# Weight staging in two buffers of 1152 columns instead of four of 576, in a two-layer hybrid recurrent decoder step

## Chip, cores and metric

The kernel runs on one core of one Trainium2 chip. The metric is the device time of one execution in microseconds (us), lower is better. The engines of the core are named as the profile names them: PE (TensorE: matrix products; PEld is its loading of weights), DVE (VectorE), ACT (ScalarE), POOL (GpSimd) and SP (SyncE, which here issues nearly all transfers). A q behind the name is the engine's queue of issued transfers and waits.

## What is computed

Two decoder layers over 576 tokens (512 of a prompt and 8 times 8 samples), model width 1024. Per layer, cut to what matters here:

```python
h = rmsnorm(x)
P = h @ W_in            # 1024 x 7952: columns of four mixers, then 4 x 1024 gate columns
o_b = mixer_b(P_b)      # four recurrent mixers (HGRN2, GLA, RWKV-7, retention), each 256 wide
x = x + W_out( sum_b sigmoid(G_b) * (o_b @ W_branch[b]) )
x = x + (silu(g) * u) @ W_ffn_out,  where g, u = split(rmsnorm(x) @ W_ffn_in)   # 2 x 2816 wide
```

All weights are float32 in HBM. The products run in float16 with a high and a low part of each operand (three products for one: high by high, high by low, low by high), so every weight tile has to be split on the chip before PE can use it.

## The kernel before

**Staging of a weight.** `wload` brings a block of weight columns (128 columns for all rows of the contraction, 8 groups of 128 rows for a contraction of 1024, 22 for `W_ffn_out`) in steps of four row groups: a tile "raw" of 128 partitions by 512 columns of float32 from the pool `wraw` (four buffers of `GW` = 576 columns), one transfer of 256 KB into it (L220), then ACT writes the high part (L228) and DVE the low part (L229) into a tile `whl` of a ring. The ring "w" has four slots of 2304 bytes a partition, one step each; the rings "rd" and "gd" have slots of 4608 bytes, two steps each. A raw buffer is free again when DVE has read it; a slot of `whl` when the last product that reads it is done.

**Products.** `gemm` (L233) runs three products for each row group; `proj` (L472) does so for the two halves of 288 tokens. A 128-column block of `W_in` is one unit: 48 products in the trace's tile `pb`.

**Order of the mixing stage.** `mix_units` lists the units: those of the mixers first, and between them two groups of eight gate units (g0, g1). `mix` runs them in order; when half 0 of a unit is through, it calls for the next unit's weights, and at each step of a unit it lets the mixers' generators (recurrences, small products) advance a little, so their work lies between the units on all engines. A gate unit m holds its block of `W_in` and, every second time, a block of `W_branch` 256 columns wide for units m and m+1 (L1445: one raw tile and one slot of "w", also used by the next unit). Its 48 `pb` products are followed by 12 products `ub` with the branch weights, and then comes the next unit's block.

**Strassen stages.** The last two gate groups (`last_gates`, eight pairs) and the feed-forward's up projection (`ffn`, blocks 3 to 21) use seven products instead of eight: four sub-blocks a11, a12, a21, a22 of 512 columns are loaded; POOL adds a22 to a21 by a transfer, then `strassen_weights` splits A11, A22, A12 and, after subtractions on POOL, S2 (in a11), S1 (a21), S3 (a22), S4 (a12), one ACT and one DVE instruction each (L1703, L1704). In `last_gates` a11 and a21 lie in raw, a12 and a22 in "w" (four transfers of 256 KB). In `ffn` an odd block lies in the two "rd" slots (two transfers of 512 KB, halves cut from them); an even block in three raw buffers and one "w" slot.

**Output projection and down projection.** `out_proj` runs blocks 0 to 3 with weights in "w", loads blocks 4 to 7 into "gd" and the feed-forward's first three block pairs (`ffn_weights`, into "w", "gs" and "r2"), while the blocks' results pass through `add_x` on DVE and ACT; `norm_half` then waits for all of them (L442). The down projection (`xb` products, 22 row groups a block) loads each block with rings ("w", "w", "w", "w", "rd").

**Who sets the order.** Each engine works its list in order. The lists are made when the kernel is built, by a scheduler that starts instructions in program order of priority as their inputs and buffers come free in its own model of the time; on the chip an instruction that waits blocks all that stand behind it on its engine.

Of the kernel before, what the change touches and what calls it, by code (L numbers as in the profile page):

```python
# [10 lines left out]
F32 = mybir.dt.float32  # L11
F16 = mybir.dt.float16
I32 = mybir.dt.int32
AF = mybir.ActivationFunctionType
# [20 lines left out]
C_RW = 64  # L35
C_GL = 128
GLA_TAU = 16.0
GW = 576
RINGS = {"u": 23, "e": 6, "gs": 6, "gt": 8, "gq": 5, "gd": 4, "rd": 2, "rs": 6, "r2": 4, "r1": 3, "rk": 2, "rq": 6, "w": 4}
SIZE = {"u": 2304, "e": 1152, "gs": 2304, "gt": 1152, "gq": 512, "gd": 4608, "rd": 4608, "rs": 2304, "r2": 2304, "w": 2304,  # L40
        "r1": 1024, "rk": 1536, "rq": 512}
PS = {"b": 4, "g": 2, "r": 2}
PACE = {"rw": ("rw", "g3", "g3", 140), "hg": ("hg", "g0", "g0", 64), "gl": ("gl", "rt", "g1", 64),
# [131 lines left out]
class Net:  # L175
    def __init__(self, ctx, tc, t):
        self.tc, self.nc, self.io = tc, tc.nc, t
        nc = self.nc

        def pool(name, bufs, **k):  # L180
            return ctx.enter_context(tc.tile_pool(name=name, bufs=bufs, **k))

        self.cp = pool("const", 1)
        self.wp = pool("wraw", 4)
        self.gp = pool("misc", 1)
        self.dr = pool("dram", 2, space=bass.MemoryType.DRAM)
        self.rings = {n: pool("ring_" + n, b) for n, b in RINGS.items()}
        self.pss = {n: pool("ps_" + n, b, space=PSUM) for n, b in PS.items()}
# [19 lines left out]
    def wload(self, pieces, nk, ncols, rings=("w",)):  # L208


        nc = self.nc
        step = GW // ncols
        tiles, parts = [], []
        for g, k0 in enumerate(range(0, nk, step)):
            kn = min(step, nk - k0)
            n = kn * ncols
            raw = self.wp.tile([128, GW], F32, tag="raw", name="raw")
            rv = raw[:, :n].rearrange("p (k c) -> p k c", k=kn)
            for ap, off, w in pieces:
                nc.sync.dma_start(out=rv[:, :, off:off + w],  # L220
                                  in_=ap[128 * k0:128 * (k0 + kn)].rearrange("(k p) c -> p k c", p=128))
            if not parts:
                ring, rings = rings[0], rings[1:] or rings
                c = SIZE[ring] // (4 * GW)
                hl = self.t(ring, [128, c, 2, GW], "whl", F16)
                parts = [hl[:, i] for i in range(c)]
            hl = parts.pop(0)
            nc.scalar.activation(hl[:, 0, :n], raw[:, :n], AF.Copy, scale=WS)  # L228
            nc.vector.scalar_tensor_tensor(hl[:, 1, :n], raw[:, :n], WS, hl[:, 0, :n], op0=MUL, op1=SUB)  # L229
            tiles.append(hl[:, :, :n].rearrange("p a (k c) -> p a k c", k=kn))  # L230
        return lambda k: (tiles[k // step][:, 0, k % step], tiles[k // step][:, 1, k % step])

    def gemm(self, ps, w, ks, c0, m, rhs, step=4):  # L233

# [1258 lines left out]
    def last_gates(self, l):  # L1493
# [3 lines left out]

        def load(bi, m):
            c = COL_GATE + 1024 * bi + 128 * m
            a = []  # L1500
            for i in range(4):
                r = [128, 4, 128]
                a.append(self.t("w", r, "sraw") if i % 2 else self.wp.tile([128, GW], F32, tag="raw", name="raw")[
                    :, :512].rearrange("p (k c) -> p k c", k=4))
                nc.sync.dma_start(out=a[i], in_=t["w_in"][l][512 * (i % 2):512 * (i % 2) + 512, c + 128 * (i // 2):c + 128 * (
                    i // 2) + 128].rearrange("(k p) c -> p k c", p=128))
            return a

        def branch(bi, m):

# [251 lines left out]
    def ffn(self, l):  # L1762
# [21 lines left out]
        def load(m):  # L1784
            q = []
            for o in (0, DFF):
                src = t["w_ffn_in"][l][:, o + 128 * m:o + 128 * m + 128]
                if m % 2:
                    a = self.t("rd", [128, KT, 128], "sraw")
                    nc.sync.dma_start(out=a, in_=src.rearrange("(k p) c -> p k c", p=128))  # L1790
                    q += [a[:, :4], a[:, 4:]]
                    continue
                for i in range(2):
                    if o and i:
                        a = self.t("w", [128, 4, 128], "sraw")
                    else:
                        a = self.wp.tile([128, GW], F32, tag="raw", name="raw")[:, :512].rearrange("p (k c) -> p k c", k=4)
                    nc.sync.dma_start(out=a, in_=src[512 * i:512 * i + 512].rearrange("(k p) c -> p k c", p=128))
                    q.append(a)
            return q  # L1800

        self.sw = {}
# [34 lines left out]
        def weights(m, rings=("w",)):  # L1837
            return self.wload([(t["w_ffn_out"][l][:, 128 * m:128 * m + 128], 0, 128)], nm, 128, rings)
# [6 lines left out]
            self.add_x(m, half, ps, l + 1 < DEPTH, l + 1 == DEPTH and m == KT - 1)  # L1845
        for m in range(6):
            self.load_x(m)
            w = weights(m, ("w", "w", "w", "w", "rd"))
            for half in range(2):
                down(m, w, half)  # L1850
        for m in (6, 7):
            self.load_x(m)
        ws = [weights(6, ("gd",)), weights(7, ("w", "w", "w", "w", "gd"))]
        if l + 1 < DEPTH:
            down(6, ws[0], 0)
            down(7, ws[1], 0)
# [97 lines left out]
```

## Time and profile before

| | us |
|---|---|
| median of three runs | 2204.15 (2200.36 to 2207.76) |
| the profiled execution | 2207.72 |
| its span, first to last instruction | 2205.9 |
| PE busy | 2039.1 |
| DVE busy | 1636.6 |
| ACT busy | 1081.3 |
| POOL busy | 682.3 |

The profile is of one execution. About 2 us of its time lie outside the span. The layers are alike in the trace: layer 0 lasts until about 1103 us and layer 1 from there on. In layer 0, mixing with its first two gate groups ends near 517 us, the last gates near 661, the output projection near 720, the up projection near 973.

### The profile page before, as it was taken

Reading aid. Unit: us, or ns where it says so; the run is one execution under the profiler, and the core shown is the slowest. Engines: PE = TensorE matmul, PEld = TensorE weight load, DVE = VectorE, ACT = ScalarE, POOL = GpSimd, SP = SyncE. Lnnn points to the kernel's source line nnn. Section 1 sums busy time; section 2 is a strip of 40 time slices with the busy share of each in tenths; the row PEclk is TensorE's granted clock in tenths of the full one; section 3 lists DMA queues with packets and bytes.
Section 4 is the critical chain, followed back from the end, with each engine's and each line's share of the span. In section 5 each row is a group of like instructions: output and inputs, shape, how many; then the busy total and the mean of one; then the engine's idle time right before and its main releaser. Section 6 shows DMA issues by size and latency. Waiting matters only on the chain.

```text
span 2205.9 us, 42236 instructions
## 1 busy us (share of the span) xinstructions
PE 2039.1 (92%) x15754; PEld 1612.3 (73%) x15754; DVE 1636.6 (74%) x3409; ACT 1081.3 (49%) x2524; POOL 682.3 (31%) x889
## 2 busy tenths in 40 slices
PE   7989999998888899999999889989998988999998
PEld 5767787786676677777777778768776766777776
DVE  7889667768785899863488986586788779998441
ACT  6554546345444555442466355453645465554332
POOL 2223222146550544320012142213465316443000
PEclk9999999999999999999999999999999999999999
DMA  6312224333435344343421222242343443443331
GB/s 181 84 41 62 58 58 110 77 83 92 116 98 177 80 116 120 87 135 103 122 68 46 58 62 60 73 111 62 87 120 88 131 141 97 111 116 87 121 106 51
DMA packets 373498, 209.59 MB, mean 95 GB/s; under 512 B 59810, under 2 KB 360410, under 8 KB 373292
## 3 DMA queue, kind: packets, MB, share of 16 engines
q1 hardware_dynamic: 365516, 192.73, 31.6%
q0 software_dynamic: 7776, 14.16, 3.6%
q8 instruction: 124, 2.03, 0.4%
q14 instruction: 82, 0.67, 0.1%
HBM read 173.72 MB, written 16.59 MB: 86 GB/s over the span
## 4 chain that ended last, share of the span: by engine, by line
PE 47%; DVE 28%; ACT 8%; issue 7%; DMA 5%; POOL 3%; SPq 1%; DVEq 0%; ACTq 0%; POOLq 0%
PE pb L243 5%; PE pb L242 5%; PE pb L241 5%; PE xb L243 4%; PE xb L242 4%; PE xb L241 4%; DVE hA L1704 4%; DVE hS L1704 3%; DVE sc L1745 2%; DVE fy L1776 2%; DVE whl L229 2%; DVE su L1745 2%; PE fsS L1731 2%; PE fsS L1729 2%; PE fsS L1730 2%
## 5 line engine op out<-in xcount | busy, mean ns | idle before, releaser
L241 PE MATMUL pb<-h,whl 128*128 128x288 f16 (+1 forms) x1504 | 435.8, 290 | 4.4 <-ACT h L464 2.2
L243 PE MATMUL pb<-h,whl 128*128 128x288 f16 (+1 forms) x1504 | 435.5, 290 | 3.2 <-DVE whl L229 3.1
L242 PE MATMUL pb<-h,whl 128*128 128x288 f16 (+1 forms) x1504 | 436.0, 290 | 0.6 <-DVE h L465 0.4
L229 DVE SCALAR_TENSOR_TENSOR whl<-raw,whl 128x512 f16<-128x512 f32 (+1 forms) x352 | 253.8, 730 | 134.3 <-ACT whl L228 132.2
L242 PEld LDWEIGHTS <-whl 128*128 128x128 f16 (+1 forms) x2784 | 275.4, 99 | 88.0 <-issue 13.5
L243 PEld LDWEIGHTS <-whl 128*128 128x128 f16 (+1 forms) x2784 | 275.1, 99 | 88.0 <-issue 12.7
L241 PEld LDWEIGHTS <-whl 128*128 128x128 f16 (+1 forms) x2784 | 277.2, 100 | 76.6 <-issue 3.6
L228 ACT ACTIVATE whl<-raw 128x512 f16<-128x512 f32 (+1 forms) x352 | 213.3, 618 | 168.2 <-PE pb L243 51.9
L243 PE MATMUL xb<-fa,whl 128*128 128x288 f16 x704 | 201.3, 286 | 0.0
L242 PE MATMUL xb<-fa,whl 128*128 128x288 f16 x704 | 201.3, 286 | 0.0
L241 PE MATMUL xb<-fa,whl 128*128 128x288 f16 x704 | 201.3, 286 | 0.0
L1729 PE MATMUL fsA<-h,hA 128*128 128x288 f16 x432 | 124.3, 288 | 14.9 <-DVE gu L1550 10.8
L1729 PE MATMUL fsS<-st,hS 128*128 128x288 f16 x456 | 132.6, 291 | 5.9 <-ACT hS L1703 5.9
L1731 PE MATMUL fsS<-st,hS 128*128 128x288 f16 x456 | 132.4, 290 | 0.4 <-DVE hS L1704 0.3
L1730 PE MATMUL fsS<-st,hS 128*128 128x288 f16 x456 | 132.5, 291 | 0.0
L1731 PE MATMUL fsA<-h,hA 128*128 128x288 f16 x432 | 124.2, 288 | 1.7 <-DVE hA L1704 1.6
L1730 PE MATMUL fsA<-h,hA 128*128 128x288 f16 x432 | 124.3, 288 | 0.0
L1707 POOL TENSOR_TENSOR raw<-raw 128x512 f32<-128x512 f32 x52 | 79.0, 1520 | 134.2 <-DVE hA L1704 129.7
L1729 PEld LDWEIGHTS <-hS 128*128 128x128 f16 x864 | 85.7, 99 | 35.9 <-ACT hS L1703 13.7
L1704 DVE SCALAR_TENSOR_TENSOR hA<-sraw,hA 128x512 f16<-128x512 f32 x110 | 103.1, 945 | 10.6 <-ACT hA L1703 10.6
L1707 POOL TENSOR_TENSOR sraw<-sraw 128x512 f32<-128x512 f32 x60 | 89.7, 1499 | 51.4 <-DVE hA L1704 45.7
L1731 PEld LDWEIGHTS <-hS 128*128 128x128 f16 x864 | 85.7, 99 | 24.8 <-DVE hS L1704 2.6
(486 smaller groups left out, 5257.8 us busy)
## 6 DMA issues: line engine op xcount, KB each, us to landing
raw<-in_w_in SPq DMA_DIRECT2D x208, 256.0 KB
sraw<-in_w_ffn_in SPq DMA_DIRECT2D x40, 512.0 KB
raw<-in_w_ffn_out SPq DMA_DIRECT2D x80, 256.0 KB
raw<-in_w_ffn_in SPq DMA_DIRECT2D x78, 256.0 KB
x<-xd SPq DMA_DIRECT2D x32, 288.0 KB
raw<-sraw POOLq DMA_DIRECT2D x34, 256.0 KB, 3.3
sraw<-in_w_in SPq DMA_DIRECT2D x32, 256.0 KB
raw<-in_w_out SPq DMA_DIRECT2D x32, 256.0 KB
```

What stands on the lines that cost most here:

```text
L228: nc.scalar.activation(hl[:, 0, :n], raw[:, :n], AF.Copy, scale=WS)
L229: nc.vector.scalar_tensor_tensor(hl[:, 1, :n], raw[:, :n], WS, hl[:, 0, :n], op0=MUL, op1=SUB)
L241: nc.tensor.matmul(ps, wh, hi, start=i == 0, stop=False)
L242: nc.tensor.matmul(ps, wh, lo, start=False, stop=False)
L243: nc.tensor.matmul(ps, wl, hi, start=False, stop=i == len(ks) - 1)
L1704: nc.vector.scalar_tensor_tensor(hl[:, 1], a, WS, hl[:, 0], op0=MUL, op1=SUB)
L1707: nc.gpsimd.tensor_tensor(dst, a, b, op=op)
L1729: nc.tensor.matmul(ps, w[a][:, 0, k], hi, start=k == 0, stop=False)
L1730: nc.tensor.matmul(ps, w[a][:, 0, k], lo, start=False, stop=False)
L1731: nc.tensor.matmul(ps, w[a][:, 1, k], hi, start=False, stop=k == 3)
L1745: nc.vector.tensor_tensor(o, a, p, op=ADD)
L1776: nc.vector.scalar_tensor_tensor(y, u, PH * AS, sg, op0=MUL, op1=MUL)
```

## The change

The staging pool has two buffers of 1152 columns instead of four of 576, and the ring "w" two slots of 4608 bytes instead of four of 2304; both take the same memory as before. `wload` takes up to 1152 columns in a step: eight row groups of 128 columns (all of a 1024-row block) in one transfer of 512 KB, and nine, nine and four row groups of `W_ffn_out` instead of five steps of four and one of two. The split is one ACT and one DVE instruction for a whole step where the ring's slot holds it ("w", "rd", "gd"), and several of 512 columns where it doesn't ("gs", "r2"). A block of `W_branch` (512 columns) stays one step, and takes a whole raw buffer and a whole slot of "w". In the Strassen stages a11 and a12 share one buffer, a21 and a22 another, each with one transfer of 512 KB: in `last_gates` one raw and one "w", in `ffn` both "rd" slots for odd blocks as before and both raw buffers for even ones. The products and the Strassen splits are the same.

```diff
-GW = 576
-RINGS = {... "w": 4}
-SIZE = {... "w": 2304,
+GW = 1152
+RINGS = {... "w": 2}
+SIZE = {... "w": 4608,
...
-        self.wp = pool("wraw", 4)
+        self.wp = pool("wraw", 2)
...
-        step = GW // ncols
-        tiles, parts = [], []
-        for g, k0 in enumerate(range(0, nk, step)):
-            kn = min(step, nk - k0)
-            n = kn * ncols
+        tiles = []
+        for k0 in range(0, nk, GW // ncols):
+            k1 = min(k0 + GW // ncols, nk)
             raw = self.wp.tile([128, GW], F32, tag="raw", name="raw")
...
-            if not parts:
-                ring, rings = rings[0], rings[1:] or rings
-                c = SIZE[ring] // (4 * GW)
-                hl = self.t(ring, [128, c, 2, GW], "whl", F16)
-                parts = [hl[:, i] for i in range(c)]
-            hl = parts.pop(0)
-            nc.scalar.activation(hl[:, 0, :n], raw[:, :n], AF.Copy, scale=WS)
-            nc.vector.scalar_tensor_tensor(hl[:, 1, :n], raw[:, :n], WS, hl[:, 0, :n], op0=MUL, op1=SUB)
+            ring, rings = rings[0], rings[1:] or rings
+            size = SIZE[ring] // 4
+            for o in range(0, k1 - k0, size // ncols):
+                kn = min(size // ncols, k1 - k0 - o)
+                hl = self.t(ring, [128, 2, size], "whl", F16)[:, :, :kn * ncols].rearrange(...)
+                src = rv[:, o:o + kn]
+                nc.scalar.activation(hl[:, 0], src, AF.Copy, scale=WS)
+                nc.vector.scalar_tensor_tensor(hl[:, 1], src, WS, hl[:, 0], op0=MUL, op1=SUB)
+                tiles += [(hl[:, 0, k], hl[:, 1, k]) for k in range(kn)]
...
 # last_gates.load
+            for i in range(2):
+                a = self.t("w", [128, KT, 128], "sraw") if i else self.wp.tile(...)[:, :1024]...
+                nc.sync.dma_start(out=a, in_=t["w_in"][l][:, c + 128 * i:c + 128 * i + 128]...)
+                q += [a[:, :4], a[:, 4:]]
...
 # ffn.load
+                a = self.t("rd", [128, KT, 128], "sraw") if m % 2 else self.wp.tile(...)[:, :1024]...
+                nc.sync.dma_start(out=a, in_=src.rearrange("(k p) c -> p k c", p=128))
+                q += [a[:, :4], a[:, 4:]]
...
-            w = weights(m, ("w", "w", "w", "w", "rd"))
+            w = weights(m, ("w", "w", "rd"))
...
-        ws = [weights(6, ("gd",)), weights(7, ("w", "w", "w", "w", "gd"))]
+        ws = [weights(6, ("gd",)), weights(7, ("w", "w", "gd"))]
```

## Rows read from the trace of the kernel before

**Rows 1.** The page: span, and busy time of each engine.

```profile
span 2205.9 us, 42236 instructions
PE 2039.1 (92%) x15754; PEld 1612.3 (73%) x15754; DVE 1636.6 (74%) x3409; ACT 1081.3 (49%) x2524; POOL 682.3 (31%) x889
```

**Rows 2.** Stretches: us, busy us (instructions) of each engine, clock, DMA share, GB/s.

```profile
250.00:350.00 100.00, 98.91 (x778) 81.28 (x776) 61.93 (x173) 45.11 (x156) 27.76 (x59) 1.00 0.24 62
660.00:720.00 60.00, 53.35 (x411) 41.10 (x409) 35.95 (x69) 29.36 (x56) 6.75 (x8) 0.94 0.56 171
760.00:850.00 90.00, 87.08 (x708) 69.01 (x706) 87.49 (x141) 47.95 (x100) 43.23 (x34) 1.00 0.44 115
972.00:1106.00 134.00, 133.84 (x1091) 106.58 (x1089) 53.79 (x102) 43.76 (x82) 1.80 (x2) 1.00 0.42 126
```

**Rows 3.** Splits by form: busy us, mean ns | idle before; the third from 250 to 300 us.

```profile
L228 ACT ACTIVATE whl<-raw 128x512 f16<-128x512 f32 x332 | 205.2, 627 | 162.4 <-PE pb L243 49.5 <-DMA raw<-in_w_ffn_out 32.6 <-PE xb L243 23.6
L228 ACT ACTIVATE whl<-raw 128x256 f16<-128x256 f32 x16 | 6.5, 406 | 3.4 <-DMA raw<-in_w_ffn_out 3.4
L229 DVE SCALAR_TENSOR_TENSOR whl<-raw,whl 128x512 f16<-128x512 f32 x11 | 7.6, 688 | 2.2 <-ACT whl L228 2.0
L229 DVE SCALAR_TENSOR_TENSOR whl<-raw,whl 128x256 f16<-128x256 f32 x16 | 6.7, 421 | 2.1 <-ACT whl L228 2.0
```

**Rows 4.** Timeline of the shortest passage from one gate unit to the next.

```profile
288.41 0.29 PE L243 MATMUL pb<-h,whl 128*128 128x288 f16 x1
...
288.79 0.63 ACT L228 ACTIVATE whl<-raw 128x512 f16<-128x512 f32 x1 [0.46 <-ACT le L1110]
...
289.45 0.69 DVE L229 SCALAR_TENSOR_TENSOR whl<-raw,whl 128x512 f16<-128x512 f32 x1 [0.20 <-ACT whl L228]
...
290.45 0.29 PE L241 MATMUL pb<-h,whl 128*128 128x288 f16 x1
```

**Rows 5.** Timeline of PE, the longest such passage: its first and last product.

```profile
320.76 0.29 PE L243 MATMUL pb<-h,whl 128*128 128x288 f16 x1
...
325.12 0.29 PE L241 MATMUL pb<-h,whl 128*128 128x288 f16 x1
```

**Rows 6.** Waits of PE, whole trace: us in total, times, longest us.

```profile
PE rps L442 <- DVE sq L436: 12.7, 3, 6.8
PE fsS L1729 <- ACT hS L1703: 12.5, 4, 3.3
PE pb L243 <- DVE whl L229: 3.1, 3, 1.3
PE pb L241 <- ACT whl L228: 2.1, 2, 1.4
```

**Rows 7.** Chain of waits, 655 to 725 us: start us, us, what.

```profile
676.64 3.60 DMA raw<-in_w_out
...
688.10 5.59 DMA raw<-in_w_ffn_in
...
695.70 3.23 DMA raw<-in_w_ffn_in
...
700.53 3.80 DMA raw<-in_w_ffn_in
...
708.55 1.34 PE rps L442 x2
```

**Rows 8.** Issues of L220 from 676.6 to 700.5 us.

```profile
L220 SPq DMA_DIRECT2D raw<-in_w_ffn_in x11: 367/367/384, 682.7 to 699.5; - x11
L220 SPq DMA_DIRECT2D raw<-in_w_out x5: 367/368/384, 676.6 to 681.7; - x5
```

**Rows 9.** Chain of waits, 925 to 960 us, and 2025 to 2042 us.

```profile
948.49 2.91 DMA raw<-in_w_ffn_out
...
951.42 0.64 ACT whl L228
...
2032.46 2.79 DMA raw<-in_w_ffn_out
```

**Rows 10.** Timeline of SP's queue, 0 to 35 us: issues.

```profile
18.42 0.33 SPq L345 DMA_DIRECT2D prow<-in_attn_norm_w  x1
...
30.70 2.78 SPq L220 DMA_DIRECT2D raw<-in_w_in  x4
```

**Rows 11.** Waits of ACT, 560 to 660 us.

```profile
ACT hA L1703 <- DMA sraw<-in_w_in: 1.4, 2, 1.0
```

More of the change, by code (lines that the diff above doesn't have):

```diff
@@ L37 @@
 GLA_TAU = 16.0
-GW = 576
-RINGS = {"u": 23, "e": 6, "gs": 6, "gt": 8, "gq": 5, "gd": 4, "rd": 2, "rs": 6, "r2": 4, "r1": 3, "rk": 2, "rq": 6, "w": 4}
-SIZE = {"u": 2304, "e": 1152, "gs": 2304, "gt": 1152, "gq": 512, "gd": 4608, "rd": 4608, "rs": 2304, "r2": 2304, "w": 2304,
+GW = 1152
+RINGS = {"u": 23, "e": 6, "gs": 6, "gt": 8, "gq": 5, "gd": 4, "rd": 2, "rs": 6, "r2": 4, "r1": 3, "rk": 2, "rq": 6, "w": 2}
+SIZE = {"u": 2304, "e": 1152, "gs": 2304, "gt": 1152, "gq": 512, "gd": 4608, "rd": 4608, "rs": 2304, "r2": 2304, "w": 4608,
         "r1": 1024, "rk": 1536, "rq": 512}
@@ L211, in wload @@
         nc = self.nc
-        step = GW // ncols
-        tiles, parts = [], []
-        for g, k0 in enumerate(range(0, nk, step)):
-            kn = min(step, nk - k0)
-            n = kn * ncols
+        tiles = []
+        for k0 in range(0, nk, GW // ncols):
+            k1 = min(k0 + GW // ncols, nk)
             raw = self.wp.tile([128, GW], F32, tag="raw", name="raw")
-            rv = raw[:, :n].rearrange("p (k c) -> p k c", k=kn)
+            rv = raw[:, :(k1 - k0) * ncols].rearrange("p (k c) -> p k c", c=ncols)
             for ap, off, w in pieces:
-                nc.sync.dma_start(out=rv[:, :, off:off + w],
-                                  in_=ap[128 * k0:128 * (k0 + kn)].rearrange("(k p) c -> p k c", p=128))
-            if not parts:
-                ring, rings = rings[0], rings[1:] or rings
-                c = SIZE[ring] // (4 * GW)
-                hl = self.t(ring, [128, c, 2, GW], "whl", F16)
-                parts = [hl[:, i] for i in range(c)]
-            hl = parts.pop(0)
-            nc.scalar.activation(hl[:, 0, :n], raw[:, :n], AF.Copy, scale=WS)
-            nc.vector.scalar_tensor_tensor(hl[:, 1, :n], raw[:, :n], WS, hl[:, 0, :n], op0=MUL, op1=SUB)
-            tiles.append(hl[:, :, :n].rearrange("p a (k c) -> p a k c", k=kn))
-        return lambda k: (tiles[k // step][:, 0, k % step], tiles[k // step][:, 1, k % step])
+                nc.sync.dma_start(out=rv[:, :, off:off + w], in_=ap[128 * k0:128 * k1].rearrange("(k p) c -> p k c", p=128))
+            ring, rings = rings[0], rings[1:] or rings
+            size = SIZE[ring] // 4
+            for o in range(0, k1 - k0, size // ncols):
+                kn = min(size // ncols, k1 - k0 - o)
+                hl = self.t(ring, [128, 2, size], "whl", F16)[:, :, :kn * ncols].rearrange("p a (k c) -> p a k c", c=ncols)
+                src = rv[:, o:o + kn]
+                nc.scalar.activation(hl[:, 0], src, AF.Copy, scale=WS)
+                nc.vector.scalar_tensor_tensor(hl[:, 1], src, WS, hl[:, 0], op0=MUL, op1=SUB)
+                tiles += [(hl[:, 0, k], hl[:, 1, k]) for k in range(kn)]
+        return lambda k: tiles[k]
     def gemm(self, ps, w, ks, c0, m, rhs, step=4):
@@ L1499, in load @@
             c = COL_GATE + 1024 * bi + 128 * m
[L1500 to L1507, printed above, removed]
+            q = []
+            for i in range(2):
+                a = self.t("w", [128, KT, 128], "sraw") if i else self.wp.tile([128, GW], F32, tag="raw", name="raw")[
+                    :, :1024].rearrange("p (k c) -> p k c", k=KT)
+                nc.sync.dma_start(out=a, in_=t["w_in"][l][:, c + 128 * i:c + 128 * i + 128].rearrange("(k p) c -> p k c", p=128))
+                q += [a[:, :4], a[:, 4:]]
+            return q
         def branch(bi, m):
@@ L1787, in load @@
                 src = t["w_ffn_in"][l][:, o + 128 * m:o + 128 * m + 128]
[L1788 to L1799, printed above, removed]
+                a = self.t("rd", [128, KT, 128], "sraw") if m % 2 else self.wp.tile([128, GW], F32, tag="raw", name="raw")[
+                    :, :1024].rearrange("p (k c) -> p k c", k=KT)
+                nc.sync.dma_start(out=a, in_=src.rearrange("(k p) c -> p k c", p=128))
+                q += [a[:, :4], a[:, 4:]]
             return q
```

## Prediction

> **What bounds the kernel.** Read the page's busy times first: PE is busy for 2039.1 of 2205.9 us, 92%, DVE for 74%, ACT for half [rows 1]. So at most 167 us are PE's idle time, and a change pays by closing gaps in PE or costs by opening them. Next, the table by stretch shows that stages differ [rows 2]: in the gate units (250 to 350 us) PE idles for 1.1 us of 100 while DVE has 38 us to spare; in the down projection (972 to 1106) it idles for 0.2 of 134; in the Strassen stage of `ffn` (760 to 850) DVE is as full as PE, 97%; around the output projection (660 to 720) PE idles for 6.7 of 60 and the transfers move most, 171 GB/s. Then the waits of PE: those for a staged weight (pb on whl) sum to 5.2 us in the whole trace, less than the 12.7 us of three waits for the sums of squares and the 12.5 us of four waits for a high part hS [rows 6]. The chains of waits show what stands behind these two: transfers into raw [rows 7, 9]. So the weights are hidden nearly everywhere now. The change keeps bytes, products and Strassen splits; it changes how late a split can begin and how long it lasts.
>
> **Durations after.** From 256 to 512 columns the ACT split grows from 406 to 627 ns, the DVE split from 421 to 688 (the row of the gate units, where POOL disturbs little) [rows 3]. The lines through these points give 1.07 us and 1.22 us for 1024 columns; a fixed part of 0.185 and 0.154 us is saved by each merged pair. The splits fall from 352 to 192 an engine (a layer has 46 blocks of `W_in`, two steps each before and one after, 8 of `W_branch` unchanged, 16 to 8 in `out_proj`, 12 to 10 in `ffn_weights`, 48 to 24 in the down projection): 160 x 0.154 = 25 us of DVE and 160 x 0.185 = 30 us of ACT.
>
> **1. Fewer instructions.** 48 of the 160 lie in the down projection, where PE has no gap to give back [rows 2]. The other 112 save 17 us of DVE in stages in which PE idles for about a tenth at most, so about a tenth of it comes through: take -2 us; bounds -17 (all of it on the path) and 0. The Trainium skill, in "VectorE: DVE Perf Modes", section on the TRN2 errata, says that operations on SBUF pay a fixed latency for each instruction and that larger tiles amortize it. The rows agree that there is a fixed part; by that rule alone the kernel would gain up to the 17 us.
>
> **2. Gate units: the cover of the split shrinks.** Before, "w" has four slots: a block takes two, the branch weights one, so one is always free for half of the next block. After, block and branch fill both slots. The next block's split can't begin until the last of the 48 products pb is done, and it needs ACT and then DVE for the whole 1024 columns before the third product can start. That is 0.04 (the wait) + 1.07 + 0.03 + 1.22 + 0.1 to PE, and between ACT's end and DVE's start some 0.3 us pass while DVE finishes another instruction (0.03 us at best, 289.42 to 289.45 [rows 4]); less the two products that need the high part alone, 0.25: about 2.5 us. The cover is what PE does from the last pb product to the next unit's first: 12 ub products and what the mixers have ready. The shortest such passage lasts 1.75 us (288.70 to 290.45) [rows 4], the longest 4.07 (321.05 to 325.12) [rows 5]. I read all 15 of layer 0: five lie under 2.5 us, at 1.75, 1.9, 2.0, 2.4 and 2.45, short by 2.0 us together; layer 1 repeats them. Scatter of half a us in ACT's and DVE's response adds about one more a layer: take +6 us for both layers. Bounds: 0, if the scheduler finds other products to put there; and 32 passages x (2.5 - 12 x 0.123, the branch products alone at the pitch of the down projection, 134 us over 1091 products [rows 2]) = +33 us. What queues behind the waiting split on ACT is the mixers' next work and the evacuation of half 1, which DVE's gate product needs. On the side of this term the Trainium skill, "Perfetto Trace Analysis", section "Optimizing Scalar/DVE Operations", says that where ScalarE and VectorE aren't saturated but cause bubbles on other engines, breaking instructions up may let work finish sooner; this is the opposite edit, in a stage where they aren't saturated [rows 2].
>
> **3. Output projection: two buffers of 512 KB in flight instead of four of 256 KB.** From 676.64 to 700.53 us, 16 transfers of 256 KB start [rows 7, 8]: 1 MB in 5.97 us. A buffer's round is landing, ACT, DVE, issue. After, landing of 512 KB isn't shown; it lies between the 3.23 us of a lone 256 KB and the 5.59 us of the slowest in a full queue [rows 7]; I take 4.4, nearer to the middle. With 1.07 + 1.22 + 0.5 of waits the round is 7.2 us for two buffers, 1 MB. The stretch has 10 blocks, 5 MB, so it can end 6 us later a layer. The late end shows today: the norm's sum starts at 708.55 [rows 7] after 12.7 us of PE waits in three places [rows 6], because `add_x` on DVE and ACT stands behind splits that wait for transfers. But the lists are made anew with the new durations, and the feed-forward weights aren't needed before 720: take +2 us a layer, +4; bounds -4 (the order puts `add_x` first) and +12.
>
> **4. First down blocks amid the Strassen products.** At 948.49 and 2032.46 us a transfer into a just freed raw buffer is waited for by ACT, behind it the next hS [rows 9]: two of the four waits in [rows 6], near 3 us each. After, block 20 holds both raw buffers until its S4 split, so down weights are staged later, past this place, and the first is needed only at 973. Take -3 (one of the two goes, or both by half); bounds -6 and, if 4.4 us of landing are waited for in place of 2.9, +3.
>
> **5. Last gates and even blocks of `ffn`.** A buffer pair is free after S4 instead of S2, one or two splits later, and lands as 512 KB. The odd blocks of `ffn` work like this already, in the stretch that is 97% busy. In the last gates only 1.4 us of ACT's waits are for these transfers [rows 11]: take +1; bounds 0 and +8 (a us for each of eight pairs).
>
> **6. Start.** The parameter rows sit in a raw buffer from 18.42 us on, and the loads of the fourth unit stand behind them on SP at 30.70 [rows 10]. With two buffers they wait for the whole second block's split instead of half of it. With that and the 5.2 us of pb waits [rows 6], which longer splits stretch: +1.5; bounds 0 and +5.
>
> The down projection costs nothing: a block's first slot is free 13 row groups, 39 x 0.123 = 4.8 us, before the next block, and nine groups are split in 1.2 + 1.4 us; DVE and ACT are busy for 40% and 33% there [rows 2]. If that cover went, 16 passages would pay 1 to 2 us each.
>
> **Sum.** -2 + 6 + 4 - 3 + 1 + 1.5 = +7.5 us against the profiled execution's 2207.72 us (span 2205.9 and 2 us around it). That execution stands 3.6 us above the median of the runs, so for a median I put 2204.2 + 7.5 = 2212.
>
> **Rivals.**
> (a) *The cover holds.* PE fills the passages with mixers' products, and the re-made lists absorb term 3. For it: ten of 15 passages are longer than 2.5 us; against it: PE's gaps there are already so small that little is ready to be moved. Terms 2 and 3 fall to 0: -2 - 3 + 2.5, about 2202.
> (b) *Faster: the fixed cost pays.* In the mixers' stretch DVE and ACT are what PE's small products wait for, and there each merged pair shortens the queue; with all of term 1 (-17), term 4 at its -6, terms 2 and 3 at half (+5) and +2.5 of the rest, -15.5: 2189; with 10 of the 17, 2196. It decides if more than half of DVE's saving comes through to PE. Against it: the saving is 1.5% of DVE's time, spread thin.
> (c) *Two buffers serialize.* A transfer can't start while both are being split, and SP, which waits in order, holds back states and stores too. Terms 2 and 3 go to their ends, +33 and +12, or to two thirds of them, with -2, -3 and +2.5 of the rest: 2231 to 2247. For it: around the output projection the transfers already move 171 GB/s and set the pace; against it: elsewhere they move 62 to 126 GB/s [rows 2].
> That the larger transfers move no faster by themselves is inside the forecast: each row of 128 columns remains a run of 512 bytes.
>
> **Chances.** What a measurement can tell from no change is about 0.3%, 6.6 us. Forecast 0.45, own range 2204 to 2222, of which 0.30 lies above 2210.8 and 0.15 within; (a) 0.20, 0.14 within and 0.06 faster; (b) 0.17, faster; (c) 0.18, slower. Faster 0.23, same 0.29, slower 0.48. The range 2192 to 2236 takes in the forecast and (a), the nearer half of (b) and a third of (c).
>
> **What would show it.** Term 2: new PE waits pb on whl (DVE, ACT) of 0.3 to 1 us between 256 and 338 and between 430 and 500 us. Term 3: the sum's wait at L442 longer than 6.8 us at the longest. Term 4: no wait for hS near 952 and 2035. Term 1: 192 splits on either engine, near 1.07 and 1.22 us. The prediction is wrong if PE's waits for whl stay near 5 us (then the cover held), if the wait at L442 shrinks, or if the down projection's stretch opens gaps.

## The result

| | before | after |
|---|---|---|
| median of four runs each, us | 2204.97 | 2232.09 (2229.36 to 2232.8) |
| ratio | | 1.0123 (95% interval 1.0103 to 1.0143) |
| the profiled execution, us | 2207.72 | 2232.7 |

The changed kernel is slower by 1.2%, 27 us. The forecast was 2212 in a range of 2192 to 2236: the direction is right, the time lies inside the range, but the sum of the terms was +7.5 us and the true one is more than three times that. It lies above the forecast's own range (2204 to 2222), at the lower end of rival (c).

The page of the profile after, busy times and the two groups of splits:

```profile
span 2230.9 us, 41166 instructions
PE 2041.7 (92%) x15754; PEld 1610.3 (72%) x15754; DVE 1622.5 (73%) x3249; ACT 1058.7 (47%) x2364; POOL 680.9 (31%) x889
...
L226 DVE SCALAR_TENSOR_TENSOR whl<-raw,whl 128x1024 f16<-128x1024 f32 (+2 forms) x192 | 225.7, 1180 | 139.1 <-ACT whl L225 139.1
L225 ACT ACTIVATE whl<-raw 128x1024 f16<-128x1024 f32 (+2 forms) x192 | 184.4, 966 | 203.5 <-PE xb L240 45.0
```

Against [rows 1], PE is busy for 2.6 us more, and its idle time grew from 166.8 to 189.2 us: the loss is idle time of PE. DVE (-14 us) and ACT (-23 us) work less, as was meant, and the kernel is slower all the same.

PE's waits after, the largest groups and those of the prediction (engine, line <- what came last: us in total, times, longest; a line number after is 3 or 4 below that of before):

```profile
PE rps L439 <- DVE sq L433: 16.7, 4, 8.3
PE gps L730 <- DVE rw_ab L720: 10.5, 2, 6.1
PE fb L238 <- DVE fy L1772: 9.4, 4, 3.6
PE fsA L1725 <- ACT bhl L1512: 9.1, 4, 2.8
PE pb L240 <- DVE whl L226: 8.8, 8, 1.8
...
PE fsS L1725 <- ACT hS L1699: 8.6, 5, 3.3
```

Against [rows 6]: PE waits 4.0 us longer for the sums of squares and 3.9 us less for hS; for staged weights (with the 3.0 us of L238 on ACT) it waits 11.8 in place of 5.2 us. The group of bhl, the split of branch weights in the last gates, is new.

**Where the 25 us went.** The nine stages are cut at products that every version has: the first pb (end of the start), the first ub (g0 begins), the 96th, 97th and 192nd ub (g0 ends, g1 begins and ends), the first ob, fb and xb, the last xb. "Last gates" holds the mixers' tail too. For each kernel profiled here, the difference from the profile before, in us, both layers added:

| kernel | start | mixers 1 | g0 | mixers 2 | g1 | last gates | output proj. | up proj. | down proj. | sum |
|---|---|---|---|---|---|---|---|---|---|---|
| before (length) | 14.1 | 469.0 | 170.6 | 182.2 | 176.5 | 293.2 | 114.4 | 507.6 | 267.2 | 2194.8 |
| after | +2.9 | +4.4 | +2.7 | +4.2 | +0.7 | +11.3 | +1.5 | -2.6 | 0 | +25.1 |
| control of before | +0.4 | -0.2 | 0 | +0.7 | -0.7 | +0.1 | -0.6 | -3.5 | 0 | -3.9 |
| control of after | +1.8 | +5.1 | +2.4 | +4.0 | +0.6 | +10.0 | +2.1 | -3.4 | 0 | +22.5 |
| "w" alone | +0.3 | +2.9 | +3.5 | -0.8 | +0.7 | +8.4 | -1.5 | -6.0 | 0 | +7.4 |
| raw alone | +2.1 | +9.1 | 0 | -1.6 | +0.8 | +8.6 | +4.1 | -6.4 | 0 | +16.7 |
| raw alone, in halves | +0.8 | +6.5 | 0 | -0.2 | -0.3 | +12.7 | +2.7 | -4.2 | 0 | +17.9 |
| after, in halves | +0.4 | +3.9 | +3.8 | +1.0 | +1.1 | +11.7 | -0.2 | -2.3 | 0 | +19.3 |
| after, splits in halves | +1.5 | +6.1 | +3.5 | -0.6 | +1.5 | +11.3 | -1.1 | +0.1 | 0 | +22.2 |
| after, transfers in halves | +2.2 | +4.0 | +2.4 | +5.1 | +0.3 | +5.0 | +2.6 | -3.5 | 0 | +18.0 |
| after, own quarters | +2.0 | +4.4 | +2.7 | +4.8 | 0 | +8.5 | +1.4 | -4.0 | 0 | +19.8 |
| before, transfers of 128 KB | -0.2 | +2.8 | 0 | -0.1 | -0.3 | -2.5 | -9.3 | -3.1 | 0 | -12.7 |
| before, five of "w" | +1.1 | +0.9 | +1.6 | +3.9 | +3.8 | +11.9 | -7.6 | +7.6 | 0 | +23.2 |
| before, five of raw | +1.2 | +4.5 | 0 | 0 | -1.8 | +7.5 | -9.9 | -7.2 | 0 | -5.6 |

These are single executions, and some stand off the medians of their kernels: that of before by 3 to 6 us, mostly in the up projection, as its control shows, and that of the changed kernel in halves by 6 us. So a column is read against the control's row, and the sum of a row can miss by this much what the medians in the next section give.

Three readings of the trace after. The start, its chain of waits (start us, us, what):

```profile
4.47 7.50 DMA raw<-in_w_in
...
11.99 1.07 ACT whl L225
...
13.08 1.23 DVE whl L226
14.31 0.38 DVE xdg L319
...
14.73 1.34 PE rps L328 x2
```

The first norm's instruction xdg stands behind the first block's split on DVE, and that waits for 512 KB beside the input's transfers. Before, the chain was 5.14, 0.64 and 0.69 us for 256 KB, and this sum started at 11.87.

The last gates of layer 0: the whole stage and two parts of it, first before, then after (us, busy us of PE, PEld, DVE, ACT, POOL, granted clock, DMA share, GB/s):

```profile
517.20:663.00 145.80, 128.75 (x993) 100.38 (x992) 116.48 (x224) 72.92 (x170) 80.69 (x81) 0.98 0.43 110
560.00:588.00 28.00, 26.42 (x190) 19.48 (x188) 20.19 (x39) 14.69 (x30) 14.48 (x16) 1.00 0.50 126
632.20:647.40 15.20, 13.42 (x109) 10.56 (x108) 13.57 (x25) 8.70 (x19) 8.74 (x7) 1.00 0.28 82
```

```profile
526.50:679.20 152.70, 132.80 (x994) 101.69 (x993) 124.44 (x221) 73.03 (x165) 80.50 (x81) 0.96 0.40 106
570.00:601.40 31.40, 28.03 (x190) 20.10 (x187) 20.19 (x39) 13.67 (x28) 15.38 (x17) 0.95 0.54 136
645.90:663.50 17.60, 14.95 (x109) 11.21 (x108) 16.49 (x27) 8.51 (x18) 8.43 (x7) 0.90 0.26 76
```

Of the 6.9 us, 2.9 are idle time of PE and 4.0 are slower products: as many of them, at a granted clock of 0.96 in place of 0.98. DVE is busy for 8 us more with three instructions fewer. The two parts hold most of the loss: 3.4 us at the end of the mixers' tail, where DVE's busy time is the same, and 2.4 us in a passage from one pair to the next. This passage, on PE's timeline after (start us, us, instruction, in brackets the idle time before it):

```profile
648.57 0.40 PE L1725 MATMUL fsA<-h,hA 128*128 128x288 f16 x1 [2.65 <-ACT bhl L1512]
...
651.40 0.44 PE L1725 MATMUL fsA<-h,hA 128*128 128x288 f16 x1
651.64 0.34 PE L1726 MATMUL fsA<-h,hA 128*128 128x288 f16 x1
651.82 0.29 PE L1727 MATMUL fsA<-h,hA 128*128 128x288 f16 x1
```

PE stood still for 2.65 us; the products behind it start 0.24 us apart instead of 0.12, the clock granted being the lower level, 1.2 GHz, until about 651.6. That adds some 1.5 us to the gap. What stands ahead on DVE at that place, and POOL's instructions beside it (timelines: start us, us, instruction):

```profile
639.80 1.62 DVE L1700 SCALAR_TENSOR_TENSOR hA<-raw,hA 128x512 f16<-128x512 f32 x1
641.35 1.76 DVE L1700 SCALAR_TENSOR_TENSOR hA<-sraw,hA 128x512 f16<-128x512 f32 x1
643.03 0.44 DVE L1741 TENSOR_TENSOR su<-sp,fsS 128x288 f32<-128x288 f32 x1
643.39 1.61 DVE L1700 SCALAR_TENSOR_TENSOR hS<-raw,hS 128x512 f16<-128x512 f32 x1
...
645.28 0.68 DVE L1700 SCALAR_TENSOR_TENSOR hS<-sraw,hS 128x512 f16<-128x512 f32 x1
```

```profile
639.60 1.27 POOL L1703 TENSOR_TENSOR raw<-sraw,raw 128x512 f32<-128x512 f32 x1 [2.10 <-DVE hA L1700]
640.95 1.60 POOL L1703 TENSOR_TENSOR raw<-raw 128x512 f32<-128x512 f32 x1
643.18 1.27 POOL L1703 TENSOR_TENSOR sraw<-sraw,raw 128x512 f32<-128x512 f32 x1 [0.62 <-DVE hA L1700]
```

The next pair's splits stand between DVE's evacuations su; those with one of POOL's subtractions beside them take 1.6 to 1.8 us, the one without 0.68.

### The profile page after: what moved, and what is told of

Read it like the earlier page. It is cut to its first block, busy times and chain, and to the rows that moved or that the text cites. A ratio compares the mean times of both kernels' runs of the same rounds, so it can differ in the third digit from the quotient of the medians.

```text
span 2230.9 us, 41166 instructions
## 1 busy us (share of the span) xinstructions
PE 2041.7 (92%) x15754; PEld 1610.3 (72%) x15754; DVE 1622.5 (73%) x3249; ACT 1058.7 (47%) x2364; POOL 680.9 (31%) x889
## 4 chain that ended last, share of the span: by engine, by line
PE 43%; DVE 31%; ACT 9%; issue 8%; POOL 5%; DMA 4%; SPq 1%; DVEq 0%; POOLq 0%; ACTq 0%
DVE hA L1700 4%; PE xb L240 4%; PE xb L239 4%; PE xb L238 4%; PE pb L239 4%; PE pb L240 4%; PE pb L238 4%; DVE hS L1700 3%; DVE whl L226 3%; DVE sc L1741 2%; DVE fy L1772 2%; DVE su L1741 2%; PE fsS L1727 2%; PE fsS L1725 1%; PE fsS L1726 1%
## 5 line engine op out<-in xcount | busy, mean ns | idle before, releaser
L238 PE MATMUL pb<-h,whl 128*128 128x288 f16 (+1 forms) x1504 | 434.4, 289 | 5.3 <-ACT whl L225 3.0
L239 PEld LDWEIGHTS <-whl 128*128 128x128 f16 (+1 forms) x2784 | 275.5, 99 | 93.1 <-issue 17.9
L238 PEld LDWEIGHTS <-whl 128*128 128x128 f16 (+1 forms) x2784 | 277.2, 100 | 77.0 <-issue 4.4
L226 DVE SCALAR_TENSOR_TENSOR whl<-raw,whl 128x1024 f16<-128x1024 f32 (+2 forms) x192 | 225.7, 1180 | 139.1 <-ACT whl L225 139.1
L225 ACT ACTIVATE whl<-raw 128x1024 f16<-128x1024 f32 (+2 forms) x192 | 184.4, 966 | 203.5 <-PE xb L240 45.0
L238 PE MATMUL xb<-fa,whl 128*128 128x288 f16 x704 | 201.3, 286 | 0.0
L1703 POOL TENSOR_TENSOR raw<-raw 128x512 f32<-128x512 f32 x70 | 105.4, 1508 | 126.1 <-DVE hA L1700 124.7
L1725 PE MATMUL fsS<-st,hS 128*128 128x288 f16 x456 | 130.4, 286 | 0.9 <-ACT hS L1699 0.9
L1727 PE MATMUL fsS<-st,hS 128*128 128x288 f16 x456 | 130.4, 286 | 0.6 <-DVE hS L1700 0.6
L1726 PE MATMUL fsS<-st,hS 128*128 128x288 f16 x456 | 130.4, 286 | 0.0
L1725 PEld LDWEIGHTS <-hS 128*128 128x128 f16 x864 | 85.7, 99 | 31.7 <-ACT hS L1699 10.0
L1700 DVE SCALAR_TENSOR_TENSOR hS<-raw,hS 128x512 f16<-128x512 f32 x104 | 96.5, 931 | 15.1 <-ACT hS L1699 14.6
L1107 ACT ACTIVATE le<-le 128x64 f32<-128x64 f32 (+2 forms) x248 | 56.6, 274 | 104.1 <-DVE le L1104 102.6
```

The costliest lines, as they stand in the source:

```text
L225: nc.scalar.activation(hl[:, 0], src, AF.Copy, scale=WS)
L226: nc.vector.scalar_tensor_tensor(hl[:, 1], src, WS, hl[:, 0], op0=MUL, op1=SUB)
L238: nc.tensor.matmul(ps, wh, hi, start=i == 0, stop=False)
L239: nc.tensor.matmul(ps, wh, lo, start=False, stop=False)
L1107: nc.scalar.activation(e, e, AF.Exp, scale=sign)
L1700: nc.vector.scalar_tensor_tensor(hl[:, 1], a, WS, hl[:, 0], op0=MUL, op1=SUB)
```

## The experiments

Theory A: the 27 us come from the buffers, namely from steps of double length (landing, splits) or from fewer, shared buffers that go free late. Rival B: from the lists, which are made anew with each edit and can fall well or badly. Medians beside their kernel before, run with them on one chip (2202.42 for the first four, then 2201.3, then 2202.04).

### "w" alone

```diff
-RINGS = {... "w": 4}   SIZE = {... "w": 2304,
+RINGS = {... "w": 2}   SIZE = {... "w": 4608,
# raw stays 4 x 576; down projection: rings "w", "w", "rd"
# last_gates: a12 and a22 as halves of one slot of "w", four transfers
+            lo = self.t("w", [128, 2, 4, 128], "sraw")
```

> Only the ring "w" is changed (two slots of 4608 bytes); raw stays four buffers of 576 columns, each with its own transfer of 256 KB and its own split into half of a slot. If the two slots of "w" are the cost, most of the 27 us is here: 2222 to 2232. If the raw buffers are (their number, and the transfers and splits of double length that they bring), this kernel stands near the one before: 2204 to 2211, with the gate units between 253 and 338 us as long as before (85.0 us, against 86.2 in the changed kernel), since the first half's split needs only 0.63 + 0.69 us after the last pb product. If the re-made lists alone decide, the time can be anything from 2190 to 2230, and the stages that lose are not the ones that lost before (mixers and last gates).

Measured: 2216.61, ratio 1.0065 (1.0050 to 1.0080), half of the loss. The gate units are longer, g0 by 3.5 us, which I had not expected here: with halves the split should have fitted under the cover. The last gates lose 8.4, the start nothing.

### Raw alone

```diff
-        self.wp = pool("wraw", 4)      # of 576
+        self.wp = pool("wraw", 2)      # of 1152, "w" stays 4 x 2304
# a step is 8 row groups: one transfer, two splits into two slots of "w"
# last_gates: a11 and a12 share a raw buffer, a21 and a22 have a slot of "w" each
```

> Only the raw pool is changed (two buffers of 1152 columns, transfers of 512 KB); "w" stays four slots of 2304 bytes, so a block's split is two ACT and two DVE instructions into two slots. If the raw buffers are the cost: 2220 to 2232, with the start still late (the first norm's sum at 13.5 us or later, against 11.87 before and 14.73 in the changed kernel; the 512 KB land at 12 us, and the first product needs only one half's split) and the last gates 4 us or more longer a layer than 149.4 us. If "w" is the cost: 2205 to 2212. If the lists alone decide: anything from 2190 to 2230.

Measured: 2224.55, ratio 1.0102 (1.0085 to 1.0118). Start late as expected (the first sum at 14.00), g0 at 0. The two parts alone cost 14 and 22 us, both together 27: they overlap.

### The changed kernel in halves

```diff
-                nc.sync.dma_start(out=rv[:, :, ...], in_=ap[128 * k0:128 * k1]...)
+                for ka in range(k0, k1, 512 // ncols): nc.sync.dma_start(...)   # 256 KB each
...
-                nc.scalar.activation(hl[:, 0], src, ...); nc.vector.scalar_tensor_tensor(hl[:, 1], src, ...)
+                for p in halves: the same two on hl[:, :, p], src[:, p]        # 512 columns each
# last_gates and even blocks of ffn: two transfers for each buffer
```

> The changed kernel's buffers (two raw of 1152 columns, two slots of 4608 bytes), but each buffer is filled by transfers of 256 KB and split by instructions of 512 columns. If the length of a transfer and of a split is the cost, this gives most back: 2206 to 2214, the start within 0.5 us of before (first norm's sum at about 12 us). If the number of buffers and the late release of a whole one is the cost, it stays at 2224 to 2236: the fixed part of 160 more splits an engine comes back, and a buffer still goes free only after both halves. If the lists alone decide: anything from 2190 to 2236.

Measured: 2220.89, ratio 1.0089 (1.0073 to 1.0105), between the two expectations. It is 18.5 us above its kernel before, so of the 27 us length costs about a third: nearly all of the start (first sum at 12.23) and most of the second mixers' stretch. Two thirds stay, with steps of the old size in shared buffers.

### A control of before

```diff
         nc.vector.memset(self.eps[:, 1:2], LN_EPS)
+        nc.vector.memset(self.eps[:, 1:2], LN_EPS)
```

> A control: the kernel before with one memset of 128 x 1 elements on VectorE, issued twice instead of once at the very start. By itself it costs under 0.1 us, but the lists of all engines are made anew from it. If the order in the lists is robust, 2202 to 2208 (no change). If re-made lists move the time by themselves, it differs from 2205 by 5 to 15 us in either direction, and a part of the 27 us of this size can't be put down to buffers.

Measured: 2202.09, ratio 0.9996 (0.9987 to 1.0005). No stage but the up projection moves by over 0.7 us. But the edit did less than I expected of it: in the trace every engine has the same instructions in the same order as before, the second memset aside. The lists were not changed, so this kernel shows how far two executions of the same lists differ, and nothing on rival B.

### Own quarters in the last gates

```diff
-            for i in range(2):   # raw: a11|a12, "w": a21|a22, one transfer each
+            for i, ring in enumerate(("raw", "r2", "w", "r2")):   # one quarter each, 256 KB each
```

> The changed kernel, but in the last gates each of the four quarters of a pair has a buffer of its own again and a transfer of 256 KB: a11 in raw, a21 in "w" (half of each left empty), a12 and a22 in "r2", which is otherwise idle in that stage but for the tail of one mixer. If two quarters that share a buffer (free only after the last split) are what makes the last gates 6.8 and 4.5 us longer, the stage from the last ub product of g1 to the first ob product comes back to within 2 us of 145.9 and 147.3 us, and the time falls by 9 to 13 us to 2219 to 2223. If that stage is longer for another reason (what the mixers left over at its start, or VectorE beside GpSimd), it stays at 150 to 153 us and the time at 2228 to 2234.

Measured: 2224.68, ratio 1.0099 (1.0081 to 1.0117): 23.4 us above its kernel before in place of 27, between the two expectations, and the last gates are still 150.2 and 151.6 us long. That two quarters share a buffer is at most a small part of that stage's loss. Nor are the wait for bhl, which is gone from this kernel, or DVE's longer durations what the stage mainly pays for: DVE is busy there for 117.47 and 116.55 us in the two layers, for 116.48 and 118.96 before.

```profile
524.90:675.10 150.20, 131.57 (x994) 101.92 (x992) 117.47 (x221) 72.60 (x165) 80.07 (x80) 0.95 0.42 107
```

### Transfers alone in halves, splits alone in halves

The two edits of the kernel in halves, one at a time.

> The changed kernel with transfers of 256 KB (two or three for a buffer), the splits whole. If the landing of 512 KB is what makes the start late, the first norm's sum starts near 12.5 us in place of 14.73 (only the longer split is left, 1.07 + 1.23 us against 0.64 + 0.69). For the whole: if the transfers' size is what the kernel with halves gained from (11 us against the changed kernel), 2219 to 2223; if the splits' length is, 2228 to 2232.

Measured: 2225.35, ratio 1.0106 (1.0090 to 1.0122).

> The changed kernel with splits of 512 columns (two or three for a buffer), the transfers whole. If the splits' length is what the kernel with halves gained from: 2219 to 2223; if the size of the transfers is: 2229 to 2234, the start still near 14 us, and DVE and ACT busy for about 14 and 20 us more than in the changed kernel.

Measured: 2226.88, ratio 1.0114 (1.0098 to 1.0131). Neither is the one cause. Above the kernel before on their own chip, both halved stand 18.5 us, transfers alone 24.1, splits alone 25.6, neither 27.1. So by the medians whole splits cost 5.6 us where the transfers are halved and 1.5 where they aren't; whole transfers 7.1 and 3.0. The interval of each ratio is some 4 us wide to either side, so 1.5 and 3.0 can't be told from nothing, and 5.6 and 7.1 hardly. The start expectation for transfers was wrong: the first sum came at 14.01, and with the splits alone halved at 13.41, so both halvings are needed there. PE's wait for rw_ab in the second mixers' stretch follows the splits' length: 7.0 us before in two places, 10.5 after; 8.9 us in the other three kernels with whole splits, 6.3 to 7.4 in all with splits of 512 columns. With the splits alone in halves:

```profile
PE gps L733 <- DVE rw_ab L723: 6.3, 2, 3.2
```

### A control of after

The memset of the control of before, in the changed kernel.

> The same control for the changed kernel: one more memset of 128 x 1 elements on VectorE at the very start, by which all lists are made anew. If the order in the lists is robust: 2229 to 2235. If some of the 27 us is an unlucky order (the sum in the mixers that waits for rw_ab, 6.1 us in place of 3.5, or the last gates), it falls by 3 to 10 us.

Measured: 2229.55, ratio 1.0124 (1.0108 to 1.0140). The loss repeats. But here too every engine has the instruction order of the changed kernel, so this is no second set of lists. What bears on rival B are the other edits: the changed kernel and the seven variants of it with two large buffers in raw, in "w" or in both each have an order of products of their own on PE, and all eight lose, 14 to 27 us.

### Raw alone, in halves

```diff
# raw alone, with two transfers of 256 KB for each buffer (last_gates and ffn too)
# splits as in raw alone: of 512 columns, but for the 32 longer ones into "rd" and "gd"
```

> Only the raw pool changed (two buffers of 1152 columns, four slots of "w"), but with transfers of 256 KB and splits of 512 columns: against the kernel before, only the release differs, since two steps share a buffer that is free after the second. If the length of the transfers is what the kernel with two large raw buffers paid for (22 us), this gives 2205 to 2212; if the shared release is, 2218 to 2225. The gate units g0 should cost nothing in either case (85.3 us a layer, four slots).

Measured: 2224.57, ratio 1.0107 (1.0091 to 1.0122), the same as with whole transfers. So in this arrangement the landing of whole transfers costs nothing, and 22 us go with two raw buffers that two steps share. That it is their late release, and not the lists made for them, is argued and not shown.

### Before with transfers of 128 KB

```diff
-                nc.sync.dma_start(out=rv[:, :, off:off + w], in_=ap[128 * k0:128 * (k0 + kn)]...)
+                for ka in range(0, kn, 256 // ncols): nc.sync.dma_start(...)   # 128 KB each
# in wload alone: the Strassen stages' own transfers keep 256 and 512 KB
```

> The kernel before with each transfer of 256 KB issued as two of 128 KB into the halves of the same buffer; splits and buffers as before. No buffer becomes scarcer, so if scarce buffers and long steps are the cause of the 27 us, this stays within 4 us of 2202, perhaps below it at the start. If the kernel before is a point to which the lists happen to fit, and any edit that re-times the loads costs the mixers and the last gates some us, it comes to 2208 to 2216, with the loss in these two stages.

Measured: 2196.63, ratio 0.9976 (0.9967 to 0.9985). Faster than both kernels. The gain is in the output projection (-9.3 in the profile), not at the start. This is against rival B in its sharp form: not every edit loses.

### One buffer more

```diff
-GW = 576
+GW = 512
# first kernel: "w": 5 slots of 2048; second kernel: "wraw": 5 buffers, "w": 4 slots of 2048
# in both, a layer's one block of 144 columns takes three steps in place of two
```

> The opposite direction: the kernel before with buffers of 512 columns in place of 576 (64 were empty in nearly all steps), and the memory that this frees spent on a fifth slot of "w". If the number of "w" slots sets the g0 units, they can't gain, since four already cover them (85.3 us); PE's waits for a staged weight, 5.2 us in all, bound the gain elsewhere in the mixers: 2196 to 2203. If the last gates gain as they lost with two slots (8 us), 2193 to 2198.

Measured: 2231.07, ratio 1.0135 (1.0117 to 1.0152). A slot more costs as much as the change under study, and in part in the same stages: 3.9 us in the second mixers' stretch and 11.9 in the last gates, but also 3.8 in g1 and 7.6 in the up projection, where the change costs 0.7 and nothing; the output projection gains 7.6. Both expectations are wrong, and so is theory A for these stages, if it says that scarcity must be the cause. For rival B it shows that new lists can cost 29 us with no buffer fewer.

> The same with the memory spent on a fifth raw buffer. If raw buffers pace the output projection and the last gates, a fifth shortens the wait for the sums of squares (12.7 us in three places) and the whole by 2 to 6 us: 2196 to 2200. If four already cover the transfers: 2200 to 2204.

Measured: 2197.06, ratio 0.9974 (0.9962 to 0.9987). The output projection gains, as expected. The last gates lose 7.5 us in this profile, but not as in the changed kernel. In layer 0, 4.2 us are one wait ahead of the output projection's first product. In layer 1, PE's idle time is that of before, and its products are slower. That wait, then the stage of layer 1 before and here:

```profile
PE ob L241 <- DVE gu L1550: 4.2, 1, 4.2
```

```profile
1598.20:1745.60 147.40, 130.92 (x995) 101.44 (x993) 118.96 (x225) 73.48 (x170) 80.23 (x78) 0.97 0.42 107
```

```profile
1599.90:1750.20 150.30, 134.04 (x993) 103.28 (x992) 118.35 (x226) 73.70 (x171) 79.81 (x76) 0.94 0.38 97
```

PE's wait for the sums of squares is longer with two raw buffers, 14.0 to 19.6 us in all eight such kernels, than with four, 5.9 to 13.1 us in five. But it isn't the fifth that shortens it: with two of raw alone, with five, and with four beside five slots of "w":

```profile
PE rps L439 <- DVE sq L433: 17.8, 3, 8.9
```

```profile
PE rps L442 <- DVE sq L436: 5.7, 5, 1.5
```

```profile
PE rps L442 <- DVE sq L436: 5.9, 4, 2.1
```

## Why the prediction was right, and where its sum was not

The direction was forecast, and most places of loss were named. That the time lies in the stated range is in part luck: it lies outside the forecast's own range, and the stated one reaches so far up for the sake of rival (c), whose mechanism the trace doesn't show. The step that failed is term 5.

**Term 1 (-2): the instructions right, the gain not seen.** The forms after, and the branch split that stands beside them:

```profile
L226 DVE SCALAR_TENSOR_TENSOR whl<-raw,whl 128x1024 f16<-128x1024 f32 x110 | 143.1, 1303 | 50.4 <-ACT whl L225 50.3
...
L1513 DVE SCALAR_TENSOR_TENSOR bhl<-braw,bhl 128x256 f16<-128x256 f32 x32 | 30.6, 960 | 2.4 <-ACT bhl L1512 2.0
```

```profile
L225 ACT ACTIVATE whl<-raw 128x1024 f16<-128x1024 f32 x110 | 115.5, 1053 | 91.3 <-PE pb L240 32.8 <-issue 17.6 <-DMA raw<-in_w_out 13.9
```

192 splits; 1.05 us on ACT for 1.07 forecast, 1.30 on DVE over all stages and 1.22 in the gate units; DVE's splits fell from 253.8 to 225.7 us and ACT's from 213.3 to 184.4, for 25 and 30 forecast. But DVE got only 14 of its 28 us back: the branch split alone grew from 20.1 to 30.6 us, now more often beside POOL (18 of 32 times for nine tenths of its time or more, 8 before). And whole splits gained the kernel nothing: by the medians they cost 1.5 to 5.6 us (above). The Trainium skill, "VectorE: DVE Perf Modes", section on the TRN2 errata, says that a large tile pays the fixed latency once and many small ones pay it each time. The splits' busy time here agrees with it, and by that rule alone the kernel would have gained. The Trainium skill, "Perfetto Trace Analysis", section "Optimizing Scalar/DVE Operations", says that breaking instructions up can finish work sooner where the two engines aren't saturated but cause bubbles. The sign of the 1.5 to 5.6 us agrees with it.

**Term 2 (+6): the place right, the size half, the symptom not.** With two slots of "w" g0 costs 2.4 to 3.8 us in all seven kernels, with four 0.0 in all six, but with five 1.6; with g1 it is +3.4 after. But in g0 no product pb waits for whl. All of PE's waits there (layer 0, after), then the longest group in g1:

```profile
PE xvp L813 <- DVE rws L865: 1.6, 2, 0.9
PE xps L847 <- ACT rxv L816: 0.2, 1, 0.2
```

```profile
PE pb L240 <- DVE whl L226: 2.2, 2, 1.8
```

In g0 PE's idle time is mixers' products that wait; of the gate units only g1 has the predicted waits for whl. That the lists put mixers' work into the passage, as rival (a) had it, fits this, and was not tested by itself. Halving the splits did not bring g0 back (3.5, 3.8), so my sum of the split's durations against the cover was not the mechanism; what goes with the loss is the two slots, however they are filled.

**Term 3 (+4): right in mechanism, +1.5 in the stage.** The sums wait 4.0 us longer, the longest 8.3 for "over 6.8", and all eight kernels with two raw buffers wait longer there than the five with four. The round: issues of 512 KB after.

```profile
694.25 1.52 SPq L218 DMA_DIRECT2D raw<-in_w_out  x2
700.67 0.37 SPq L218 DMA_DIRECT2D raw<-in_w_out  x1
702.88 0.37 SPq L218 DMA_DIRECT2D raw<-in_w_ffn_in  x1
707.38 0.37 SPq L218 DMA_DIRECT2D raw<-in_w_ffn_in  x1
710.58 0.37 SPq L218 DMA_DIRECT2D raw<-in_w_ffn_in  x1
714.34 2.76 SPq L218 DMA_DIRECT2D raw<-in_w_ffn_in  x2
```

Six issues, 3 MB, in the 20.1 us from 694.25 to 714.34: 6.7 us per MB, for 7.2 forecast and 5.97 before [rows 7, 8].

**Term 4 (-3): right, and spent again in the same stage.** The waits for hS near 952 and 2035, 2.8 and 3.1 us, are down to 0.5 us in each layer. The Strassen part of the up projection, from the last product fb on, is 6 to 8 us a layer shorter (layer 0, before, then after):

```profile
765.10:972.90 207.80, 198.81 (x1597) 156.64 (x1597) 196.66 (x335) 103.56 (x221) 87.16 (x67) 0.99 0.42 109
```

```profile
786.40:988.50 202.10, 196.99 (x1596) 155.77 (x1595) 192.49 (x328) 102.63 (x214) 84.49 (x66) 1.00 0.44 113
```

This part lasts 200.0 to 202.2 us in both layers of all eight kernels with two raw buffers, and 205.0 to 210.0 in the five with four; both layers added, after stands 10 us below the control of before, more than my bound of -6. But the blocks ahead of it take 11 us longer. In each layer there is a new wait of 3.6 us, fb for fy on DVE, which stands behind Strassen splits; one of 3.2 to 3.6 us is in all kernels with two raw buffers, and in that with five slots of "w". So the whole stage's -2.6 is no better than the control's -3.5.

**Term 5 (+1, bounds 0 to +8): the step that failed.** "In the last gates only 1.4 us of ACT's waits are for these transfers: take +1." The transfers are indeed not what is waited for, yet the stage lost 11.3 us (10.0 in the control of after), the largest share: no wait for a transfer was taken for no cost. I priced a buffer's release and its landing, and not what the new lists put ahead of the instruction that PE waits for, nor the clock, which makes a gap of 2.65 us cost over 4. Of the 11.3 us, 5.9 are idle time of PE (39.4 in place of 33.5 us) and 5.4 slower products. What sets this off is not settled. DVE's durations, longer beside POOL, are part of it at most: own quarters undo them and bring back 2.8 us. Halved transfers bring back 6.3. Both halvings bring back nothing (11.7), but that profile is the one 6 us above its median, and its idle time, 37.2 us, is that of halved transfers, 37.0. Of the kernels with one buffer more, that with five slots of "w" loses 11.9 with 42.4 us of idle time, so fewer buffers aren't needed for such a loss. What would tell is a kernel with the instruction order of before and the buffers of after; it wasn't tried.

**Term 6 (+1.5): the place right, +2.9 (+1.8 in the control), another mechanism.** Not the parameter rows but the first block: 7.50 us landing in place of 5.14, splits of 1.07 and 1.23 us, and the norm behind them.

**No term: the mixers, +8.6.** I counted only stretched pb waits, within term 6. In the second stretch (+4.2) the four kernels with whole splits have +4.0 to +5.1, the five variants with halves -1.6 to +1.0; the kernel with five slots of "w" has +3.9 with splits of 512 columns, from a cause that isn't known. In the first stretch the edits scatter from -0.2 to +9.1, and nothing here tells the change's +4.4 from that.

**Down projection: costs nothing, right,** to 0.0 us in every kernel.

**The rivals.** (a) fell by its time. (b) fell: the saving was made and did not reach PE. (c) gave the time, 2231 to 2247, but not by its mechanism: gate units and output projection cost 3.4 and 1.5 us, not 33 and 12.

## What to carry to other kernels

A saving on engines that don't set the end need not reach it: 28 us less of splits on DVE gained nothing here. What counts is what now stands ahead of the instruction that PE waits for, so price a merged step by the in-order queues that it lengthens, in every stage. Two large buffers were not four small ones, even where no transfer is waited for: raw alone lost 22 us with transfers of the old size. When the sum of the terms misses, cut both traces at the same products, stage by stage, and let single-part kernels fill the table. A control that is to make the lists anew has to be compared with them in the trace: both of these left every engine's order as it was. And try the opposite edit, since smaller transfers and a fifth raw buffer, not larger ones, gained 0.25%.

## What the runs showed of the hardware

One form of DVE split, 128 x 512, took 0.68 us alone and 1.61 to 1.76 us beside one of POOL's subtractions (rows above). Over the whole trace after, this Strassen split took 0.68 us in the mean of the 207 that ran with no POOL instruction beside them, and 1.17 us in that of the 72 that had one for nine tenths of their time or more. The branch split of 256 columns shows the same in the mean: 632 ns before, 960 after, for 421 ns of this size where POOL is idle, in the down projection [rows 3].

A gap of PE of 2.65 us was followed by the lower clock, 1.2 GHz, for some 3 us. The length of the gap alone doesn't decide this. The same wait of 3.64 us stands in both layers after; in layer 0 the granted clock of the 4 us behind it was 1.00, in layer 1 0.50, and half as many products ran in them:

```profile
783.28 0.28 PE L238 MATMUL fb<-h,whl 128*128 128x288 f16 x1 [3.64 <-DVE fy L1772]
...
1874.85 0.40 PE L238 MATMUL fb<-h,whl 128*128 128x288 f16 x1 [3.64 <-DVE fy L1772]
```

```profile
783.28:787.28 4.00, 4.00 (x33) 3.21 (x33) 3.15 (x6) 1.77 (x5) 1.27 (x1) 1.00 0.81 225
1874.85:1878.85 4.00, 4.00 (x17) 2.52 (x17) 2.73 (x5) 1.47 (x4) 1.27 (x1) 0.50 0.79 225
```

And one slot more in a ring, with buffers of 512 columns, made the kernel 1.35% slower, as much as the whole change.
